# Seven block products instead of eight in a third chunk of each feed-forward part, with weight splits and sums 2048 columns wide

## The chip, the cores and the metric

The kernel runs on one core of a Trainium2 chip, as one program. The core has a matrix engine (TensorE, PE in the profile; its weight loads are listed as PEld), a vector engine (VectorE, DVE), a scalar engine (ScalarE, ACT), GpSimd (POOL) and SyncE (SP), which here issues nearly all loads from memory. Each engine runs its own instructions in their order and waits for others on semaphores. The metric is the device time of one execution in microseconds; smaller is better.

## The reference, cut to what matters

256 tokens of 1024 channels in float32 pass through two stacks. The first has four layers, each a mixer (convolution, pooling, attention, convolution) and a feed-forward part; the second has two layers, each a feed-forward part, a mixer and another feed-forward part. So there are eight feed-forward parts, all of this form (in the second stack the two input matrices are the halves of one):

```
y = rms_norm(x, g)                       # 256 x 1024
f = (silu(y @ w_gate) * (y @ w_up)) @ w_down
x = x + rms_norm(f, g2)                  # halved in the second stack
# w_gate, w_up: 1024 x 2816;  w_down: 2816 x 1024
```

All products have to be as good as float32.

## The kernel before, in words

**Three matmuls for one.** Every weight and activation is split into a hi part, rounded to the matrix engine's reduced float32 format, and a lo part, which is the rest. `mm3` (line 279) is one step: hi by hi, hi by lo, lo by hi, three matmuls of 128 rows, 128 columns of weights from the activation and 512 moving columns (lines 282, 283 and 284). The activations are the stationary side, the split weights the moving one, so the first of the three matmuls reads the weight's hi part, the second its lo part.

**Units.** Weights come as raw tiles of 128 x 2048 float32 (1 MB, one load each). A unit is a raw tile that is to be split: ScalarE copies it to the hi tile (line 229), VectorE subtracts hi from raw into the lo tile (line 190). Each is done in two halves of 1024 columns, so a unit is two copies and two low parts. hi, lo and raw tiles come from one set of 19 buffers (`r8`). In a feed-forward part two hold the split activations and two the split sums of activations, which leaves 15.

**Seven products.** A feed-forward part walks the 2816 hidden columns in six chunks, five of 512 columns and one of 256; in the code they are numbered c = 0 to 5, here they are the first to the sixth. For one chunk, the 1024 input channels fall into two halves, the weights into gate and up, the tokens into two halves of 128: a 2 x 2 block product with blocks b11 (gate, first channels), b12 (up, first), b21 (gate, second) and b22 (up, second). Done plainly (`both`, from line 547, for the second and the fourth chunk) that is eight block products of 4 steps, 32 steps. In the chunks named in `SUMS` (`seven`, from line 582, the third and the fifth) it is done after the scheme of Strassen and Winograd with seven: b11, b21, t1 = b11 + b12, t2 = t1 + b22, b22, t3 = b12 + b22, t4 = t2 + b21, each by an activation block or a sum of activation blocks (made once a part by `x_sums`). That is 28 steps. The sums t1 to t4 are made by VectorE on the raw tiles, in place (`pre_add`, line 170, the additions in line 181): t1, t2 and t4 one after the other on the tile of b11, t3 on the tile of b12. A raw tile can't be added to before the low part of the last unit that was split from it has been issued (line 175). Each of these seven is a unit of its own; a chunk of eight products has four units, since each weight unit serves both token halves.

Between these products stand the steps of the chunk before through `w_down`: 16 steps from two units (d, first and second half; the four calls of `down` in `seven`, interleaved in `both`). The results are taken out of the accumulators by small operations 512 columns wide: in a chunk of seven, three copies and two silu on ScalarE and, on VectorE, an addition for gate 0 (L605), an addition and a product for up 0 (L612, L615), an addition for up 1 (L622) and a product for gate 1 (L630). The hidden values are transposed on the matrix engine (L511) and split (L291 on ScalarE, L292 on VectorE), once for each token half. In a chunk of eight it is L566 and L571 instead of those five.

**What sets the order.** A planner writes the instructions of all engines in one order. `tick` is called after each step and calls `split_step` (line 196), which issues at most the next half unit. It does nothing while its own estimate of VectorE's backlog is over 1.5 steps (`vector`, line 156: one step for 640 columns, with 60 columns added for each operation). Units are taken strictly in order. Before it splits unit i it tries the sum of unit i+1 (lines 206 to 210). It stops, and flushes the low parts that are still to be issued, when unit i is too far ahead of the products (`ahead`), when `limit` units are split and not used up, or when fewer than two buffers are free. Otherwise the low part of a half is issued when the next half has been copied (`flush(1)`). A product whose unit isn't split yet forces it (`need`, `force=True`). `load_step` issues the load of the next raw tile when more than two buffers are free and fewer than three loaded tiles are waiting.

Of the kernel before, what the change touches and what calls it, by code (L numbers as in the profile page):

```python
# [25 lines left out]


ORD = "VQKvco"
SUMS = (2, 4)


class Slots:
# [18 lines left out]
class Core:  # L51
    def __init__(self, ctx, tc, I, out):
        self.tc, self.nc, self.I, self.out = tc, tc.nc, I, out
        P = lambda name, **kw: ctx.enter_context(tc.tile_pool(name=name, bufs=1, **kw))
        sb = P("sb")
        self.sb = sb
        self.r8 = Slots(sb, "r8_", 19, W8, F32R)
        self.r2 = Slots(sb, "r2_", 6, 512, F32R)
        self.f2 = Slots(sb, "f2_", 10, 512, F32)
        self.gn = Slots(sb, "gn_", 2, D, F32)  # L60
        self.ps = Slots(P("ps", space=PSUM), "ps_", 8, 512, F32)
        self.dram = P("dram", space=DRAM)
        self.small_pool = sb
        self.n_small = 0
        self.later = []
        self.ticks = 0
        self.tasks = []
        self.pieces = []
        self.n_dma = self.n_split = 0
        self.sub = 0  # L70
        self.cur, self.ahead = -1, 2
        self.limit = 6
        self.live = 0
        self.raw, self.hl, self.xt = {}, {}, {}
        self.units, self.lows = [], deque()
        self.begun, self.waiting, self.n_low = set(), 0, 0
        self.uses, self.summed = [], set()
        self.vector_until = 0.0
        self.z = {}
        self.raw_max = 3  # L80
        self.spare = 2
        self.reserve = 0
        self.hold = 0
        self.rr, self.nr = {}, {}
        self.pre_gains = deque()
        self.gains, self.gq = deque(), deque()
# [83 lines left out]
    def pre_add(self, i):  # L170

        src, first = self.units[i]
        if first is None or i in self.summed:
            return True
        if src not in self.raw or first not in self.raw or any(self.units[j][0] == src for j in range(self.n_low, i)):
            return False
        self.begin(src)
        self.begin(first)
        a, b = (self.view(self.raw[n], src) for n in (src, first))
        for sl in (slice(0, 2), slice(2, 4)):  # L180
            self.nc.vector.tensor_tensor(out=a[:, sl], in0=a[:, sl], in1=b[:, sl], op=ALU.add)  # L181
            self.vector(1024)
        self.used(first)
        self.summed.add(i)
        return True

    def flush(self, keep=0):
        while len(self.lows) > keep:
            lo, raw, hi, eng, i, last = self.lows.popleft()
            eng.tensor_tensor(out=lo, in0=raw, in1=hi.bitcast(F32), op=ALU.subtract)  # L190
            self.vector(1024)
            if last:
                self.n_low = i + 1
                self.used(self.units[i][0])
# [1 line left out]
    def split_step(self, force=False, eng=None):  # L196
# [27 lines left out]
            self.begin(src)  # L224
        hi, lo = (self.view(t, src) for t in self.hl[i])
        k = hi.shape[1]
        sl = slice(0, k // 2) if self.sub == 0 else slice(k // 2, k)
        raw = self.view(self.raw[src], src)[:, sl]
        self.nc.scalar.copy(out=hi[:, sl], in_=raw)  # L229
        self.lows.append((lo[:, sl], raw, hi[:, sl], eng or self.nc.vector, i, self.sub == 1))  # L230
        self.flush(1)
        self.n_split += self.sub
        self.sub ^= 1
        self.load_step()
        return True

# [258 lines left out]
    def ffn(self, plan, half, nxt):  # L495
        G, Dn = plan
        nc = self.nc
        self.limit, self.reserve, self.ahead = 7, 2, 4
        self.join(self.xt[0])
        xT, rr = self.xT, {0: self.rr[0]}  # L500
        acc = {}
# [190 lines left out]
        for c in range(1, 5):  # L692
# [7 lines left out]
            if c == 3 and nxt == "pool":  # L700
                self.band = self.r8.get(F32)
                nc.sync.dma_start(out=self.band[:, 0:1568], in_=self.band_dram)
        self.ahead = 2
        down(4, 0)
        self.limit, self.ahead = 6, 4
        gate_up(5, 0)
# [1024 lines left out]
```

## Time and profile before

| | us |
|---|---|
| median of 3 runs | 2119.83 (2119.67 to 2119.86) |
| profiled execution | 2119.03 |
| its span, first to last instruction | 2116.5 |
| PE busy | 2090.4 |
| VectorE busy | 1559.2 |
| ScalarE busy | 1211.7 |
| mean granted clock of TensorE, as a share of full speed | 0.999 |

The profile is of one execution. Its times count from the first instruction, so a place in it is given by its microsecond. Matmuls are pipelined and a record of one overlaps the next (0.40 us long, 0.23 us from start to start); the same holds, for less than a tenth of a microsecond, for the operations of VectorE and ScalarE. So the work of an engine is counted here from start to start. In a row, "x5" is five instructions of one form one after the other, "[1.11 <-ACT r L229]" is 1.11 us in which the engine stood before it and what ended that: here ScalarE's line 229. Tile names are without their numbers: r is any buffer of weights or activations, ps an accumulator, f a buffer of 512 columns.

### The profile page before, as it was taken

The numbers are of one execution on the slowest core, as the hardware profiler recorded it, in microseconds if no ns is written. First come the engines' busy times: TensorE is split into PE (matmuls) and PEld (weight loads), VectorE is DVE, ScalarE is ACT, GpSimd is POOL, SyncE is SP. The second block draws the span as 40 slices with busy tenths as digits, with TensorE's granted clock in tenths as the row PEclk, the third lists the DMA queues.
The fourth block names the chain that finished last, engine by engine and source line by source line (L and its number), as shares of the span: only waits on it lengthen the run. The fifth ranks groups of instructions, "written<-read, shape, count | busy, mean of one in ns | idle before, by whom it ended". The sixth has DMA issues, their size and how long they took to land. (4 is left out here: it accounts for less than half of the span.)

```text
span 2116.5 us, 24989 instructions
## 1 busy us (share of the span) xinstructions
PE 2090.4 (99%) x9653; PEld 1688.8 (80%) x9653; DVE 1559.2 (74%) x2016; ACT 1211.7 (57%) x1742; POOL 76.9 (4%) x130
## 2 busy tenths in 40 slices
PE   9999999999999999999999999999999999999998
PEld 6877777888888788887888887878888888787887
DVE  6678678875677776688877774787778776479775
ACT  5566455655665455556555456775556555667553
POOL 1000000000000000000000001010000001000000
PEclk9999999999999999999999999999999999999999
DMA  8556544555444564545555464344564545344442
GB/s 299 192 176 222 185 170 173 205 184 207 140 168 171 189 238 161 187 169 199 206 184 182 152 236 156 120 150 171 207 227 160 209 183 177 133 165 160 179 165 94
DMA packets 175622, 383.74 MB, mean 181 GB/s; under 512 B 10428, under 2 KB 29116, under 8 KB 175504
## 3 DMA queue, kind: packets, MB, share of 16 engines
q1 hardware_dynamic: 172592, 372.04, 49.5%
q0 software_dynamic: 2624, 9.58, 1.3%
q8 instruction: 76, 1.25, 0.2%
q10 hardware_dynamic: 288, 0.52, 0.1%
q14 instruction: 42, 0.34, 0.0%
HBM read 380.28 MB, written 1.84 MB: 181 GB/s over the span
## 5 line engine op out<-in xcount | busy, mean ns | idle before, releaser
L282 PE MATMUL ps<-r,r 128*128 128x512 f32 (+2 forms) x2752 | 1103.0, 401 | 3.6 <-ACT r L291 2.5
L283 PE MATMUL ps<-r,r 128*128 128x512 f32 (+2 forms) x2752 | 1082.0, 393 | 5.3 <-DVE r L190 3.9
L284 PE MATMUL ps<-r,r 128*128 128x512 f32 (+2 forms) x2752 | 1083.0, 394 | 3.1 <-DVE r L292 3.0
L190 DVE TENSOR_TENSOR r<-r,r 128x1024 fp32r<-128x1024 f32 (+1 forms) x797 | 934.2, 1217 | 164.5 <-ACT r L229 161.1
L229 ACT CAST r<-r 128x1024 fp32r<-128x1024 f32 x798 | 791.7, 1043 | 386.7 <-DVE r L181 160.7
L284 PEld LDWEIGHTS ps<-r,r 128*128 128x128 f32 (+1 forms) x2752 | 515.6, 187 | 128.7 <-DVE r L292 9.3
L283 PEld LDWEIGHTS ps<-r,r 128*128 128x128 f32 (+1 forms) x2752 | 516.7, 188 | 120.4 <-DVE r L190 8.6
L282 PEld LDWEIGHTS ps<-r,r 128*128 128x128 f32 (+1 forms) x2752 | 516.8, 188 | 116.0 <-ACT r L291 3.2
L181 DVE TENSOR_TENSOR r<-r,r 128x1024 f32<-128x1024 f32 x128 | 150.9, 1220 | 61.7 <-DMA r<-in_ffn_w_in_dram 31.8
L291 ACT CAST r<-ps 128x512 fp32r<-128x512 f32 (+1 forms) x108 | 59.9, 554 | 150.3 <-PE ps L511 142.1
L292 DVE TENSOR_TENSOR r<-ps,r 128x512 fp32r<-128x512 f32 (+1 forms) x108 | 69.6, 647 | 88.2 <-ACT r L291 88.2
L571 DVE SCALAR_TENSOR_TENSOR f<-ps,rr,f 128x512 f32<-128x512 f32 x32 | 23.9, 748 | 70.0 <-PE ps L284 70.0
L291 ACT CAST r<-f 128x512 fp32r<-128x512 f32 x84 | 51.4, 619 | 37.3 <-DVE f L376 22.2
L312 POOL TENSOR_TENSOR st<-st,c_mhalf 128x1 f32<-128x1 f32 x28 | 15.9, 569 | 1547.2 <-DVE st L311 1546.8
L316 ACT ACTIVATE c_junk<-x 128x512 bf16<-128x512 f32 x56 | 35.3, 631 | 54.8 <-DVE x L349 53.9
L292 DVE TENSOR_TENSOR r<-f,r 128x512 fp32r<-128x512 f32 x84 | 57.6, 709 | 5.6 <-ACT r L291 3.5
L511 PEld LDWEIGHTS ps<-c_ident,f 128*128 128x128 f32 x352 | 44.3, 140 | 13.0
L511 PE MATMUL ps<-c_ident,f 128*128 128x128 f32 x352 | 54.0, 272 | 0.0
L376 DVE TENSOR_TENSOR f<-ps,c_pre 128x512 f32<-128x512 f32 x52 | 33.7, 686 | 22.7 <-PE ps L302 22.1
L349 DVE SCALAR_TENSOR_TENSOR x<-f,st,x 128x512 f32<-128x512 f32 x56 | 39.6, 749 | 2.5 <-POOL st L312 0.9
L316 ACT ACTIVATE c_junk<-ps 128x512 bf16<-128x512 f32 x52 | 31.0, 597 | 17.0 <-PE ps L284 16.2
L341 DVE TENSOR_TENSOR f<-ps,gn 128x512 f32<-128x512 f32 x52 | 35.5, 683 | 6.7 <-ACT c_junk L316 6.7
(193 smaller groups left out, 933.8 us busy)
## 6 DMA issues: line engine op xcount, KB each, us to landing
r<-in_ffn_w_in_dram SPq DMA_DIRECT2D x80, 1024.0 KB, 5.4
r<-in_ffn_w_down_dram SPq DMA_DIRECT2D x44, 1024.0 KB, 6.3
r<-in_ffn_w_out_dram SPq DMA_DIRECT2D x44, 1024.0 KB, 7.1
r<-in_ffn_w_gate_dram SPq DMA_DIRECT2D x40, 1024.0 KB, 5.1
r<-in_ffn_w_up_dram SPq DMA_DIRECT2D x40, 1024.0 KB, 5.3
r<-in_mix_w_in_dram SPq DMA_DIRECT2D x28, 1024.0 KB, 5.0
r<-in_conv_w_in_dram SPq DMA_DIRECT2D x22, 1024.0 KB, 5.8
r<-in_attn_w_qkv_dram SPq DMA_DIRECT2D x12, 1024.0 KB, 5.1
```

The source lines that it names most:

```text
L181: self.nc.vector.tensor_tensor(out=a[:, sl], in0=a[:, sl], in1=b[:, sl], op=ALU.add)
L190: eng.tensor_tensor(out=lo, in0=raw, in1=hi.bitcast(F32), op=ALU.subtract)
L229: self.nc.scalar.copy(out=hi[:, sl], in_=raw)
L282: mm(out=out, lhsT=x[0], rhs=w[0], start=first, stop=False, skip_group_check=more)
L283: mm(out=out, lhsT=x[0], rhs=w[1], start=False, stop=False, skip_group_check=more)
L284: mm(out=out, lhsT=x[1], rhs=w[0], start=False, stop=last, skip_group_check=more)
L291: self.nc.scalar.copy(out=hi, in_=src)
L292: self.nc.vector.tensor_tensor(out=lo, in0=src, in1=hi.bitcast(F32), op=ALU.subtract)
L316: self.nc.scalar.activation(out=self.junk[:, 0:src.shape[-1]], in_=src, func=ACTF.Square, scale=scale, accum_out=acc)
L341: mul = lambda n: nc.vector.tensor_tensor(out=mg[n], in0=src[n], in1=g[:, n * 512:(n + 1) * 512], op=ALU.mult)
L349: nc.vector.scalar_tensor_tensor(out=xs, in0=mg[n], scalar=r, in1=xs, op0=ALU.mult, op1=ALU.add)
L511: nc.tensor.transpose(out=b[:, j * 128:(j + 1) * 128], in_=s[:, j * 128:(j + 1) * 128], identity=self.ident)
```

## The change

The fourth chunk (c = 3) joins `SUMS`, so the third, fourth and fifth chunks are all done with seven products; the order of loads and units of the fourth follows from the same code. `pre_add` makes a sum with one addition of 2048 columns instead of two of 1024. A new flag `whole` is set at the start of each feed-forward part and cleared after its fifth chunk; while it is set, a unit that is begun by the planner, and not forced by a product, is split with one copy and one low part of 2048 columns. A forced unit is still split in two halves. The estimate of VectorE's backlog counts the real width.

```diff
@@ -26,7 +26,7 @@
 
 
 ORD = "VQKvco"
-SUMS = (2, 4)
+SUMS = (2, 3, 4)
 
 
 class Slots:
@@ -76,6 +76,7 @@
         self.begun, self.waiting, self.n_low = set(), 0, 0
         self.uses, self.summed = [], set()
         self.vector_until = 0.0
+        self.whole = False
         self.z = {}
         self.raw_max = 3
         self.spare = 2
@@ -177,9 +178,8 @@
         self.begin(src)
         self.begin(first)
         a, b = (self.view(self.raw[n], src) for n in (src, first))
-        for sl in (slice(0, 2), slice(2, 4)):
-            self.nc.vector.tensor_tensor(out=a[:, sl], in0=a[:, sl], in1=b[:, sl], op=ALU.add)
-            self.vector(1024)
+        self.nc.vector.tensor_tensor(out=a, in0=a, in1=b, op=ALU.add)
+        self.vector(2048)
         self.used(first)
         self.summed.add(i)
         return True
@@ -188,7 +188,7 @@
         while len(self.lows) > keep:
             lo, raw, hi, eng, i, last = self.lows.popleft()
             eng.tensor_tensor(out=lo, in0=raw, in1=hi.bitcast(F32), op=ALU.subtract)
-            self.vector(1024)
+            self.vector(raw.shape[1] * raw.shape[2])
             if last:
                 self.n_low = i + 1
                 self.used(self.units[i][0])
@@ -224,13 +224,15 @@
             self.begin(src)
         hi, lo = (self.view(t, src) for t in self.hl[i])
         k = hi.shape[1]
-        sl = slice(0, k // 2) if self.sub == 0 else slice(k // 2, k)
+        whole = self.whole and self.sub == 0 and not force
+        sl = slice(0, k) if whole else slice(0, k // 2) if self.sub == 0 else slice(k // 2, k)
         raw = self.view(self.raw[src], src)[:, sl]
         self.nc.scalar.copy(out=hi[:, sl], in_=raw)
-        self.lows.append((lo[:, sl], raw, hi[:, sl], eng or self.nc.vector, i, self.sub == 1))
+        self.lows.append((lo[:, sl], raw, hi[:, sl], eng or self.nc.vector, i, whole or self.sub == 1))
         self.flush(1)
-        self.n_split += self.sub
-        self.sub ^= 1
+        if not whole:
+            self.sub ^= 1
+        self.n_split += self.sub == 0
         self.load_step()
         return True
 
@@ -496,6 +498,7 @@
         G, Dn = plan
         nc = self.nc
         self.limit, self.reserve, self.ahead = 7, 2, 4
+        self.whole = True
         self.join(self.xt[0])
         xT, rr = self.xT, {0: self.rr[0]}
         acc = {}
@@ -701,6 +704,7 @@
                 self.band = self.r8.get(F32)
                 nc.sync.dma_start(out=self.band[:, 0:1568], in_=self.band_dram)
         self.ahead = 2
+        self.whole = False
         down(4, 0)
         self.limit, self.ahead = 6, 4
         gate_up(5, 0)
```

## Rows read from the trace of the kernel before

**Rows 1.** The page, part 1: engine, busy us (share of the span), instructions.

```profile
PE 2090.4 (99%) x9653; PEld 1688.8 (80%) x9653; DVE 1559.2 (74%) x2016; ACT 1211.7 (57%) x1742; POOL 76.9 (4%) x130
```

**Rows 2.** Waits, matmuls and weight loads: who waited for whom, us, times, longest.

```profile
PE ps L283 <- DVE r L190: 3.9, 7, 1.3
...
PEld ps L283 <- DVE r L190: 8.6, 12, 1.7
```

**Rows 3.** Windows, fifth part: PE, PEld, DVE, ACT, POOL busy (instructions); clock, DMA, GB/s.

```profile
1106.03:1140.29 34.26, 34.26 (x154) 27.72 (x152) 24.56 (x26) 15.46 (x19) 0.00 (x0) 1.00 0.43 148
1140.29:1171.87 31.58, 31.58 (x144) 25.67 (x142) 28.98 (x29) 23.31 (x27) 0.00 (x0) 1.00 0.57 205
1171.87:1206.40 34.53, 34.46 (x154) 27.69 (x152) 22.00 (x21) 12.55 (x14) 0.00 (x0) 1.00 0.49 178
1206.40:1237.98 31.58, 31.58 (x144) 25.66 (x143) 28.95 (x29) 23.31 (x27) 0.00 (x0) 1.00 0.58 207
```

**Rows 4.** Timeline, matmuls, third chunk: start, us, engine, line, what, [idle before].

```profile
1140.29 0.48 PE L282 MATMUL ps<-r,r 128*128 128x512 f32 x1
...
1157.46 0.40 PE L282 MATMUL ps<-r,r 128*128 128x512 f32 x1
1157.69 0.40 PE L283 MATMUL ps<-r,r 128*128 128x512 f32 x1
...
1171.87 0.39 PE L282 MATMUL ps<-r,r 128*128 128x512 f32 x1
```

**Rows 5.** Timeline, VectorE, third chunk.

```profile
1141.19 0.69 DVE L292 TENSOR_TENSOR r<-ps,r 128x512 fp32r<-128x512 f32 x1 [1.33 <-ACT r L291]
1142.14 1.23 DVE L190 TENSOR_TENSOR r<-r,r 128x1024 fp32r<-128x1024 f32 x1 [0.25 <-ACT r L229]
...
1148.81 0.68 DVE L605 TENSOR_TENSOR f<-ps,f 128x512 f32<-128x512 f32 x1
1149.41 1.21 DVE L190 TENSOR_TENSOR r<-r,r 128x1024 fp32r<-128x1024 f32 x1
1151.74 1.23 DVE L190 TENSOR_TENSOR r<-r,r 128x1024 fp32r<-128x1024 f32 x1 [1.11 <-ACT r L229]
...
1155.15 5.76 DVE L190 TENSOR_TENSOR r<-r,r 128x1024 fp32r<-128x1024 f32 x5
...
1161.55 0.75 DVE L615 SCALAR_TENSOR_TENSOR f<-f,rr,f 128x512 f32<-128x512 f32 x1
1162.22 0.68 DVE L622 TENSOR_TENSOR f<-ps,f 128x512 f32<-128x512 f32 x1
1162.82 6.89 DVE L190 TENSOR_TENSOR r<-r,r 128x1024 fp32r<-128x1024 f32 x6
```

**Rows 6.** Timelines, VectorE (first row) and ScalarE, around the start of the third chunk.

```profile
1134.57 2.36 DVE L181 TENSOR_TENSOR r<-r,r 128x1024 f32<-128x1024 f32 x2 [2.07 <-DMA r<-in_ffn_w_in_dram]
...
1135.91 2.11 ACT L229 CAST r<-r 128x1024 fp32r<-128x1024 f32 x2 [10.50 <-DVE r L181]
1140.57 0.59 ACT L291 CAST r<-ps 128x512 fp32r<-128x512 f32 x1 [2.55 <-PE ps L511]
1141.05 2.00 ACT L229 CAST r<-r 128x1024 fp32r<-128x1024 f32 x2
```

**Rows 7.** Timeline, first chunk of the fifth part, its fourth unit.

```profile
1088.70 5.79 ACT L229 CAST r<-r 128x1024 fp32r<-128x1024 f32 x6
...
1090.46 5.77 DVE L190 TENSOR_TENSOR r<-r,r 128x1024 fp32r<-128x1024 f32 x5
...
1091.74 0.19 PEld L283 LDWEIGHTS ps<-r,r 128*128 128x128 f32 x1 [0.33 <-DVE r L190]
```

**Rows 8.** Windows, third and fifth chunk of the first part.

```profile
168.20:201.20 33.00, 31.92 (x144) 25.62 (x142) 27.55 (x28) 22.28 (x27) 0.00 (x0) 1.00 0.62 223
236.70:268.80 32.10, 31.94 (x143) 25.61 (x142) 26.61 (x27) 21.09 (x25) 0.00 (x0) 1.00 0.63 225
```

**Rows 9.** Windows, the start.

```profile
10.00:20.00 10.00, 9.07 (x36) 7.29 (x37) 8.23 (x11) 6.35 (x14) 2.27 (x2) 0.83 0.86 290
```

## The prediction

> **What bounds the kernel now.** I read the page's busy shares first, then the waits of the matrix engine, then the stretches of one feed-forward part, then its timelines. The busy shares show PE at 99% and DVE at 74% [rows 1]: the matrix engine sets the time, and the vector engine looks as if it had a quarter of the span to spare. The waits agree: over the whole run the matmuls of line 283, the first that read a low part, waited 3.9 us for VectorE, and their weight loads 8.6 us [rows 2]. So a matmul less is time gained, as long as the weights are split in time.
>
> The average hides two kinds of stretch. I take the fifth feed-forward part, which starts at 1081.85. Its chunks of eight products (second and fourth) last 34.26 and 34.53 us with VectorE busy 24.56 and 22.00; its chunks of seven (third and fifth) last 31.58 with VectorE busy 28.98 and 28.95 [rows 3]. A chunk of seven leaves VectorE 2.6 us, a chunk of eight 10 to 12. The kernel now alternates the two, and what the one overdraws the other pays back.
>
> **How much lead is left.** In the third chunk VectorE starts at 1141.19 and is nearly gapless until 1162.82, where the fourth chunk's first split begins [rows 5]. The first half of unit t3's low part ends at 1152.97, and its second, the first of the five low parts from 1155.15, at 1156.4; t3's product starts at 1157.46 and wants the second half two steps (1.4 us) later [rows 4, 5]. That is 2.5 us of margin, the least of the chunk. The fourth chunk's first low part is complete at 1162.82 + 2 x 1.14 = 1165.1, against its use at 1171.87: a lead of 7 us. Today a chunk of eight follows and rebuilds it. After the change a chunk of seven follows, and then another.
>
> **The change, part by part.**
>
> *One product less in the fourth chunk.* It drops 4 steps of 3 matmuls. Starts are 0.23 us apart [rows 4], so 12 x 0.232 = 2.8 us; the two stretches measured differ by 34.53 - 31.58 = 2.95 [rows 3]. I take 2.95 a part, bounds 2.7 and 3.1; eight parts: -23.6 us. It lies on PE and is real if nothing waits.
>
> *What VectorE gets for it.* Three more weight units to split and four sums, so 9 splits and 4 sums in each of three chunks, beside seven small operations: five of 0.60 and two of 0.67 by their spacing [rows 5], 4.3 us. A 1024-wide low part follows the one before by (5.76 - 1.22)/4 = 1.135 us, a 512-wide operation by 0.60 [rows 5]. So 512 more columns cost 0.535, and 2048 wide should take 1.135 + 1.07 = 2.21, against 2.27 for two halves. Bounds 2.14 (0.07 less again) and 2.27. Thirteen of them are 28.7 us; with the small ones 33.0 us in a chunk in which PE needs 31.6. Already without any idle time VectorE is 1.4 us a chunk too slow.
>
> *What the width costs.* In halves the second half of a sum runs while ScalarE copies the first: the sums start at 1134.57, the first copy at 1135.91, 0.11 after the first half [rows 6]; the low part follows with no wait for the copy. With one sum, one copy and one low part each waits for the whole of the one before. A copy 1024 wide takes (5.79 - 1.05)/5 = 0.95 by spacing [rows 7], one 512 wide 0.48 [rows 6], so 2048 should take 1.88 by spacing and 1.97 by its record. From the earliest next start on VectorE (0.08 before the sum's record ends) to the low part: 0.08 + 0.11 + 1.97 + 0.04 = 2.2 us. The 0.04 is the gap from the first of the copies from 1141.05, with 1.05, to the low part of 1142.14 [rows 5, 6]. This hole comes at t1 and at t2, where it can't be filled: t2 is summed in place on the tile from which t1 was summed, so its sum waits for t1's low part (line 175), and the planner takes units strictly in order, so nothing but a small operation can stand there. t3 and t4 are summed one unit ahead and have no hole. Two holes a chunk, 0 to 2.2 us each; I take the whole, since the durations are measured and only the order is inferred, but in the fifth chunk I let small operations stand in the holes at no cost.
>
> *Third to fourth chunk, added up on VectorE's queue in the fifth part.* Start 1141.19; three small 1.8, then seven wide (sum t3, first down unit, b22, sum t4, t3, second down unit, t4) 15.5: 1158.5. Then 1.3 for the half-0 up value, b11 2.2, up value of half 1 0.6 (its product ends at 1160.3), b21 2.2, sum t1 2.2: 1167.0. Hole 2.2, t1 2.2, small 0.6, sum t2 2.2, hole 2.2, t2 2.2, small 0.7: 1179.3. Sum t3 2.2, down unit 2.2, small 0.6, b22 2.2, small 0.6, sum t4 2.2, t3 2.2: 1191.5. PE wants it 17.4 us into the chunk (17.17 in the third chunk, and 0.23 because the hi part alone feeds the first matmul): 1171.87 + 17.4 = 1189.3 [rows 4]. Late by 2.2, so PE stands 2.2 us.
>
> *Fourth to fifth chunk.* From t3 to the next t3: 13 wide 28.7, small ones outside the holes 3.1, holes 4.4: 36.2 against 31.6 of PE. Late by another 4.6. Together 6.8 us a part, 54 us in eight. Bounds: without holes VectorE is 2.2 us early in the fourth chunk and never late: 0. With 2.27 for a wide one and everything else as above: 8.7. I stay at 6.8.
>
> Here the Trainium skill has two rules side by side, in "Perfetto Trace Analysis", section "Optimizing Scalar/DVE Operations": larger operations help an engine that is saturated, since each pays some 60 ns of access on VectorE, and breaking operations up helps one that is not saturated but makes bubbles on others. The rows agree with the first (0.06 us saved a pair); by that rule alone the sum would have no holes and come out some 54 us lower. The second rule speaks against this change, and the holes above are what it would mean here.
>
> *The width at the start of a part.* In the first chunk the fourth unit is split late: its copies start at 1088.70, its first half low part at 1090.46, and the weight load at 1091.74 already waited 0.33 us for it [rows 7]. One whole low part would start after a copy of 1.97, at 1090.7, and end at 1093.0 instead of 1091.6: 1.3 us later, less 0.1 that today's second half costs. I take 1.2 a part, 9.6 in all; bounds 0 (the unit is forced and stays in halves) and 2.2.
>
> *The first part.* Its chunks of seven already take 33.00 and 32.10 us instead of 31.58 [rows 8], because VectorE has more to do there. I add 2 us, bounds 0 and 4.
>
> *The rest costs nothing.* Bytes and number of weight loads are the same, and ScalarE needs 9 x 1.9 + 4 = 21 us in a chunk of 31.6. The evacuations of the seven products replace those of the eight and are in the 4.3 us.
>
> **The sum.** -23.6 + 54.4 + 9.6 + 2 = +42.4 us. The profiled execution took 2119.03 us, 0.8 under the median of the runs shown, so 2119.0 + 42.4 = 2161.4; against the median it would be 2162.2. I say 2162.
>
> **Rivals.**
>
> *Faster: the holes are filled.* If the planner, short of a free buffer, flushes b11's low part before it takes b21, t1 is summed one unit early and b21's low part stands in the first hole. Buffers are short: 15 of the 19 are left for weights, and a chunk of seven holds four raw tiles. Against it: with VectorE late, PE frees buffers first. With both holes covered nothing waits: -23.6 and 0 to 9.6, so 2095 to 2105; with one of two filled, half the hole time goes (2.2 us in the fourth chunk, 2.2 in the fifth): 6.8 - 4.4 = 2.4 a part, and with the start 2119.0 + 8 x (2.4 + 1.2 - 2.95) = 2124, less where the start costs less. I put the rival at 2100, the middle of the first two.
>
> *Slower still: the raw weights come late.* The sum of t2 waited 2.07 us for its load [rows 6]. If in the fourth and fifth chunks b22 finds a buffer only when the third chunk's last down unit is done, VectorE waits there too: 2 x 2.07 x 8 = 33 us more, 2195. Against it: late VectorE means that loads have had longer.
>
> *The clock.* Standing still can lower the granted clock: in the stretch from 10 to 20 us it is 0.83, the only one of those shown below 1.00 [rows 9], so 3.4 us went at the lower of 1.2 and 2.4 GHz, which costs 1.7. After each of some sixteen stalls: 27 us more, 2189. Against it: the waits of the first part left its chunks at 1.00 [rows 8]. The Trainium skill, "TensorE: Matmul & The Clock Gate", section "Why this matters for your kernels", has the rule that idle gaps between bursts of matmuls bring the clock down; the trace neither shows nor excludes it for gaps of 2 us amid dense work.
>
> **How the numbers follow.** The forecast has 0.58, the filled holes 0.27 for faster and 0.05 for about even (one hole in two filled and a little less at the start), late loads 0.07, the clock 0.03. What a measurement of this kernel can tell from no change is 0.2%, 4.2 us. So faster 0.27, same 0.05, slower 0.68. The range reaches down into the filled holes, to 2102, and up to 2185, which is 8 x (8.7 + 2.2 - 2.95) + 2 above 2119: the wide operations at 2.27 and the start at 2.2. The likeliest case's own range is 2135 to 2185; its lower end is wide operations of 2.14, which take 2.2 of the 6.8 away, and a start that costs nothing: 8 x (4.6 - 2.95) + 2.
>
> **What would show it.** Right: a fourth-chunk stretch of 31.6 us of matmuls that lasts 33 to 35, a fifth of 35 to 37, matmul waits for line 190 of some 50 us in all instead of 3.9, VectorE waiting 2.1 us for the copy at t1 and t2, a wide low part of 2.2 by spacing. Wrong: chunks of 31.6 us three times in a row, or a first chunk no longer than today's.

## The result, and the profile after

The changed kernel takes 2195.59 us (median of 4 runs, 2193.85 to 2196.38) against 2119.85 for the kernel before: 1.0356 times as long, 95% interval 1.0344 to 1.0369. The forecast was 2162 in a range of 2102 to 2185. The direction was right, the time lies above the range.

Lines have moved a little: the low part is still L190, the weight copy L229 is L230, the second matmul L283 is L285, and L601, L628, L630 and L292 are L604, L631, L633 and L294. The page, part 1, of the kernel after:

```profile
PE 2100.8 (96%) x9557; PEld 1678.4 (77%) x9557; DVE 1672.2 (76%) x1761; ACT 1235.0 (56%) x1519; POOL 76.9 (4%) x130
```

96 matmuls are gone, yet PE's share fell from 99 to 96% [rows 1]: it waits. The waits of the kernel after (who for whom: us in total, times, longest):

```profile
PEld ps L285 <- DVE r L190: 70.4, 62, 2.3
...
PE ps L285 <- DVE r L190: 47.5, 36, 2.0
...
PE ps L284 <- ACT f L604: 25.0, 26, 1.5
```

The matmuls' wait for low parts, 3.9 us before [rows 2], is 47.5. The second wait, for L604 (the copies of the products out of the accumulators), is new. Where it happens, by the windows of the fifth part, first to fifth chunk (columns as in [rows 3]):

```profile
1116.00:1141.35 25.35, 24.14 (x109) 19.03 (x109) 21.20 (x25) 15.62 (x20) 2.21 (x4) 1.00 0.45 152
1141.35:1175.59 34.24, 34.24 (x152) 27.71 (x152) 23.21 (x18) 14.84 (x13) 0.00 (x0) 1.00 0.41 148
1175.59:1207.17 31.58, 31.58 (x143) 25.70 (x142) 29.52 (x19) 18.65 (x15) 0.00 (x0) 1.00 0.56 200
1207.17:1242.91 35.74, 32.64 (x141) 25.33 (x141) 30.58 (x19) 19.12 (x15) 0.00 (x0) 1.00 0.48 177
1242.91:1281.66 38.75, 35.26 (x141) 27.38 (x141) 30.09 (x20) 21.20 (x18) 0.00 (x0) 0.91 0.47 163
```

The second and third chunks last as long as before [rows 3]. The first is 1.17 us longer (24.18 before), the fourth, which lost four steps, 1.21 longer instead of 2.95 shorter, the fifth 7.17 longer. From this stretch, free of waits, of 31.58 to those of 35.74 and 38.75 the stall is 4.2 and 7.2 us: 11.3 a part. The eight parts are longer by 8.2 to 11.8 us each, which accounts for the 75 us.

What happens on VectorE is seen at the border of the third to the fourth chunk. VectorE, kernel after (start, us, line, [idle before and what ended it]):

```profile
1200.14 2.29 DVE L181 TENSOR_TENSOR r<-r,r 128x2048 f32<-128x2048 f32 x1
1204.45 2.29 DVE L190 TENSOR_TENSOR r<-r,r 128x2048 fp32r<-128x2048 f32 x1 [2.03 <-ACT r L230]
1206.66 0.69 DVE L294 TENSOR_TENSOR r<-ps,r 128x512 fp32r<-128x512 f32 x1
1207.26 2.28 DVE L181 TENSOR_TENSOR r<-r,r 128x2048 f32<-128x2048 f32 x1
1212.15 0.75 DVE L633 SCALAR_TENSOR_TENSOR f<-f,rr,f 128x512 f32<-128x512 f32 x1 [2.61 <-ACT f L631]
1212.82 2.28 DVE L190 TENSOR_TENSOR r<-r,r 128x2048 fp32r<-128x2048 f32 x1
1215.02 2.28 DVE L181 TENSOR_TENSOR r<-r,r 128x2048 f32<-128x2048 f32 x1
1217.22 2.28 DVE L190 TENSOR_TENSOR r<-r,r 128x2048 fp32r<-128x2048 f32 x1
1219.43 0.68 DVE L608 TENSOR_TENSOR f<-ps,f 128x512 f32<-128x512 f32 x1
1221.37 0.69 DVE L294 TENSOR_TENSOR r<-ps,r 128x512 fp32r<-128x512 f32 x1 [1.26 <-ACT r L293]
```

ScalarE at the same place:

```profile
1209.63 1.91 ACT L230 CAST r<-r 128x2048 fp32r<-128x2048 f32 x1 [4.73 <-DVE r L181]
1211.44 0.68 ACT L631 ACTIVATE f<-ps,rr 128x512 f32<-128x512 f32 x1
1212.02 3.70 ACT L230 CAST r<-r 128x2048 fp32r<-128x2048 f32 x2
```

L181 is the sum of t1, then of t2, and at 1215.02 of t3. The hole before t1's low part, 2.03, is the wait of 2.1 that was forecast. In the hole before t2's stands a small operation (L633), but it doesn't fill the hole: VectorE stands 2.61 us before it, for the silu of L631, which is on ScalarE's queue behind the very copy (1209.63) that t2's low part needs. t2's low part starts 5.56 us after its sum, of which 2.2 are the sum. At 1221.37 another small operation (L294, the low part of a hidden value) adds a wait of 1.26.

### The profile page after: what moved, and what is told of

It reads as the page before. It is cut to its first block, busy times and chain, and to the rows that moved or that the text cites. A ratio compares the mean times of both kernels' runs of the same rounds, so it can differ in the third digit from the quotient of the medians.

```text
span 2191.9 us, 24366 instructions
## 1 busy us (share of the span) xinstructions
PE 2100.8 (96%) x9557; PEld 1678.4 (77%) x9557; DVE 1672.2 (76%) x1761; ACT 1235.0 (56%) x1519; POOL 76.9 (4%) x130
## 4 chain that ended last, share of the span: by engine, by line
PE 70%; DVE 19%; issue 5%; ACT 4%; DMA 1%; POOL 1%; DVEq 0%; SPq 0%; POOLq 0%; ACTq 0%
PE ps L285 21%; PE ps L286 21%; PE ps L284 21%; DVE r L190 11%; DVE r L181 5%; ACT r L230 2%; PE ps L304 2%; PE ps L514 1%; ACT r L293 1%; DVE r L294 1%; PE ps L1334 1%; ACT c_junk L318 1%; PE ps L1410 1%; ACT f L631 0%; DVE f L378 0%
## 5 line engine op out<-in xcount | busy, mean ns | idle before, releaser
L285 PE MATMUL ps<-r,r 128*128 128x512 f32 (+1 forms) x2720 | 1079.1, 397 | 50.2 <-DVE r L190 47.5
L284 PE MATMUL ps<-r,r 128*128 128x512 f32 (+1 forms) x2720 | 1098.6, 404 | 26.5 <-ACT f L604 25.0
L190 DVE TENSOR_TENSOR r<-r,r 128x2048 fp32r<-128x2048 f32 (+2 forms) x550 | 964.4, 1787 | 162.0 <-ACT r L230 159.9
L286 PE MATMUL ps<-r,r 128*128 128x512 f32 (+1 forms) x2720 | 1074.5, 395 | 0.1
L230 ACT CAST r<-r 128x2048 fp32r<-128x2048 f32 (+2 forms) x551 | 805.3, 1501 | 394.1 <-DVE r L181 289.2
L285 PEld LDWEIGHTS ps<-r,r 128*128 128x128 f32 x2720 | 514.0, 189 | 178.9 <-DVE r L190 70.4
L284 PEld LDWEIGHTS ps<-r,r 128*128 128x128 f32 x2720 | 514.2, 189 | 150.3 <-ACT f L604 38.1
L286 PEld LDWEIGHTS ps<-r,r 128*128 128x128 f32 x2720 | 512.9, 189 | 120.7 <-DVE r L294 3.9
L181 DVE TENSOR_TENSOR r<-r,r 128x2048 f32<-128x2048 f32 x96 | 219.4, 2285 | 22.6 <-DMA r<-in_ffn_w_in_dram 11.8
L294 DVE TENSOR_TENSOR r<-ps,r 128x512 fp32r<-128x512 f32 (+1 forms) x108 | 69.7, 648 | 91.4 <-ACT r L293 91.1
L294 DVE TENSOR_TENSOR r<-f,r 128x512 fp32r<-128x512 f32 x84 | 57.5, 709 | 4.2 <-ACT r L293 2.1
L633 DVE SCALAR_TENSOR_TENSOR f<-f,rr,f 128x512 f32<-128x512 f32 x24 | 18.0, 750 | 41.8 <-ACT f L631 41.8
L611 ACT ACTIVATE f<-f,rr 128x512 f32<-128x512 f32 x24 | 17.4, 724 | 52.2 <-DVE f L608 52.2
L604 ACT COPY f<-ps 128x512 f32<-128x512 f32 x72 | 41.0, 584 | 7.7 <-PE ps L286 7.7
```

Source lines behind the costliest of these rows:

```text
L181: self.nc.vector.tensor_tensor(out=a, in0=a, in1=b, op=ALU.add)
L284: mm(out=out, lhsT=x[0], rhs=w[0], start=first, stop=False, skip_group_check=more)
L285: mm(out=out, lhsT=x[0], rhs=w[1], start=False, stop=False, skip_group_check=more)
L286: mm(out=out, lhsT=x[1], rhs=w[0], start=False, stop=last, skip_group_check=more)
L294: self.nc.vector.tensor_tensor(out=lo, in0=src, in1=hi.bitcast(F32), op=ALU.subtract)
L604: nc.scalar.copy(out=f[n], in_=b)
```

## The experiments

Times are medians; each ratio is to the kernel before in the same session, with its 95% interval.

**1. The third seven alone, in halves.**

```diff
 # the kernel before
-SUMS = (2, 4)
+SUMS = (2, 3, 4)
```

> Only the third chunk of seven is added to the kernel before; splits and sums stay in halves of 1024 columns. Theory A (VectorE is the bound, and it is the width that puts holes in its queue at t1 and t2: the sum, the copy and the low part of 2048 columns stand one after the other, and small operations that wait for ScalarE's queue lengthen the hole): without holes VectorE needs 13 x 2.27 + 4.3 = 33.8 us a chunk against 31.6, and is about in time up to the fifth chunk; each part gains 2.95 us and loses 0 to 3 again, so 2096 to 2116, middle 2108. Rival B (three chunks of seven in a row overload VectorE by themselves and the width is neutral but for the first chunk): the fourth and fifth chunks stall by 4 and 7 us as after the change, so 2185.

2186.15 us, 1.0311 (1.0296 to 1.0327). My theory A was that the wide operations make the holes and halves do without; it fell, and the time is rival B's 2185. The windows of its fifth part, third to fifth chunk:

```profile
1173.21:1204.78 31.57, 31.57 (x143) 25.69 (x142) 28.43 (x28) 19.52 (x23) 0.00 (x0) 1.00 0.56 200
1204.78:1238.86 34.08, 32.05 (x141) 25.43 (x140) 31.41 (x32) 19.18 (x23) 0.00 (x0) 1.00 0.57 196
1238.86:1278.01 39.15, 33.35 (x142) 25.13 (x140) 30.86 (x30) 19.48 (x23) 0.00 (x0) 1.00 0.50 179
```

The stall is there without one wide operation (2.5 + 7.6), and with the clock at 1.00. Two groups of its page (busy, mean ns of one | idle before, what ended most of it):

```profile
L283 PE MATMUL ps<-r,r 128*128 128x512 f32 (+1 forms) x2720 | 1076.1, 396 | 73.1 <-DVE r L190 71.6
L282 PE MATMUL ps<-r,r 128*128 128x512 f32 (+1 forms) x2720 | 1092.6, 402 | 4.6 <-ACT f L601 1.9
```

In this kernel the matmuls wait 71.6 us for low parts and 1.9 for the copies of L601; in the kernel after it was 47.5 and 25.0, together 72.5. By these totals the wait for those copies, behind wide weight copies on ScalarE's queue, took the place of a wait for VectorE and added next to nothing; the third experiment tests it.

**2. The width alone.**

```diff
 # the kernel after
-SUMS = (2, 3, 4)
+SUMS = (2, 4)
```

> Only the width is added to the kernel before; the fourth chunk keeps eight products. Theory A: the first chunk gets 1.2 us longer in each part (9.6 in all, a little more in the last part), the chunks of seven keep their 31.6 because the chunk of eight before each of them gives the lead back; 2129 to 2131. Rival B: the same. Rival C (the wide copies stand in front of the evacuations on ScalarE, and the matmuls wait for line 604 in any chunk of seven): 25 us of such waits in 24 chunks, so some 17 in 16: 2145 or more.

2129.42 us, 1.0044 (1.003 to 1.0058): +9.6. The first chunk of the fifth part takes 25.41, the chunks of seven stay at 31.6. The width costs 1.2 us at the start of each part and nothing in a seven that follows an eight.

**3. Is it VectorE's load or ScalarE's?** Each sum adds 128 of its 2048 columns.

```diff
 # the kernel after
-        self.nc.vector.tensor_tensor(out=a, in0=a, in1=b, op=ALU.add)
+        self.nc.vector.tensor_tensor(out=a[:, 0, 0:128], in0=a[:, 0, 0:128], in1=b[:, 0, 0:128], op=ALU.add)
```

> The kernel after, but each of the four sums of a chunk adds only 128 of its 2048 columns; the other columns of t1 to t4 are the unsummed blocks, so the result is another. The order is the same, and ScalarE's work is the same. Theory A: VectorE has 4 x 2.1 us less in a chunk, 24.6 us against 31.6, so no chunk of seven stalls: 2119 - 23.6 + 9.6 = 2106, 2104 to 2112. Rival C (ScalarE's queue holds up the matmuls): its copies and evacuations are as many as before, so most of the waits for line 604 stay, and the time stays above 2140.

2102.76 us, 0.9917 (0.9897 to 0.9936), a little under theory A's 2104. The windows of its fourth and fifth chunks in the fifth part:

```profile
1162.50:1194.00 31.50, 31.50 (x142) 25.56 (x141) 23.77 (x19) 18.88 (x15) 0.00 (x0) 1.00 0.56 201
1194.00:1225.80 31.80, 31.80 (x142) 25.55 (x141) 23.05 (x19) 20.13 (x16) 0.00 (x0) 1.00 0.58 199
```

ScalarE does as much as before, and in these chunks TensorE waits for nothing. The planner still counts 2048 columns a sum, and from the first to the fifth chunk of all eight parts the instructions of VectorE and of ScalarE stand in the same order as in the kernel after, so VectorE's load alone is changed. The stall needs the sums' time on VectorE. The matmuls' wait for L604 goes from 25.0 to 0.9 us with it.

**4. Wide from the second chunk on.**

```diff
 # the kernel after, ffn
-        self.whole = True          # ahead of the first chunk
...
+        self.whole = True          # after gate_up(0, 1)
```

> The kernel after, but the first chunk of each part is split in halves as before; the width begins with the second chunk. If the 1.2 us by which each first chunk grew come from the one wide split of its fourth unit, the time falls by 9.6 us and up to 2 more in the last part: 2184 to 2187. If they come from elsewhere (the sum of the fourth chunk, later loads), it stays at 2195.

2182.8 us, 1.0294 (1.0279 to 1.031). The first chunk is back at 24.19, and the whole is 12.8 us shorter, a little more than the 9.6 to 11.6 expected. Against halves everywhere (first experiment) the wide operations are worth 3.4 us: after the first chunk the width is about neutral for the whole time.

**5. Two sevens in a row.**

```diff
 # the kernel before
-SUMS = (2, 4)
+SUMS = (2, 3)
```

> The kernel before with its two chunks of seven side by side (third and fourth); the fifth has eight products; all in halves. As many matmuls, splits and sums as before, only the neighbourhood is changed. Theory D (VectorE's account: a chunk of seven costs it as much work as PE has time, and each us in which it stands idle in such a run of chunks comes out as a stall; a chunk of eight pays back): the fourth chunk stalls by 2.5 us as in the run with three chunks in halves, the fifth not; 8 x 2.5 above 2120, 2136 to 2144. Rival (the stall comes from where the fifth chunk stands, at the hand-over to the sixth, not from a row of sevens): no more than 2 us a part in the fourth, and the time within 2120 to 2128.

2144.86 us, 1.0118 (1.0103 to 1.0133), just over what was expected. The number of matmuls is the same as before; the order alone costs 25 us. In the fifth part the fourth chunk takes 34.10 instead of 31.6, the chunk of eight behind it 0.9 more than the 34.2 that such a chunk takes without waits, and the sixth 0.4 more. The window of the fourth chunk:

```profile
1184.77:1218.87 34.10, 32.05 (x142) 25.42 (x141) 31.39 (x32) 21.08 (x25) 0.00 (x0) 1.00 0.61 214
```

**6. Two sums on GpSimd.**

```diff
 # the first experiment, pre_add
+            if i in self.on_pool:      # t3 and t4
+                self.nc.gpsimd.tensor_tensor(out=a[:, sl], in0=a[:, sl], in1=b[:, sl], op=ALU.add)
```

> Three chunks of seven in halves, with the sums for t3 and t4 (issued one unit ahead) on GpSimd instead of VectorE, which has 4 x 1.14 = 4.5 us less in a chunk. GpSimd took 2.36 us for a 1024-wide subtraction in the kernel before, so 9.4 us a chunk, beside VectorE. Theory D: about 11 us less work in the 88 us that VectorE took from the start of the third chunk to t3 of the fifth, against 8.3 us by which it was late: hardly a stall is left, 2094 to 2106. Rival E (the two engines get in each other's way in the buffers, and VectorE's operations get longer beside GpSimd's): the saving is eaten up, 2140 to 2190, and VectorE's 1024-wide records grow well beyond 1.22 us. Rival F (ScalarE's order, not VectorE's load): no more than 15 us better than the 2186 in halves.

2264.94 us, 1.0678 (1.0662 to 1.0694): the rival was right, and by more than it said. Groups of this run (busy, mean ns of one):

```profile
L196 DVE TENSOR_TENSOR r<-r,r 128x1024 fp32r<-128x1024 f32 x841 | 1114.3, 1371 | 149.9 <-ACT r L235 145.6
...
L185 POOL TENSOR_TENSOR r<-r,r 128x1024 f32<-128x1024 f32 x96 | 300.4, 3151 | 748.6 <-DMA r<-in_ffn_w_in_dram 284.3 <-DMA r<-in_ffn_w_up_dram 186.9 <-PE ps L290 108.8
```

A low part of 1024 columns, 1217 ns on average in the first experiment, takes 1371. 841 of them are 130 us more of VectorE, while the sums taken away were 117. The average mixes two kinds. Two low parts on VectorE, and the two GpSimd additions beside them (start, us):

```profile
1209.23 6.19 DVE L196 TENSOR_TENSOR r<-r,r 128x1024 fp32r<-128x1024 f32 x2
1207.65 6.69 POOL L185 TENSOR_TENSOR r<-r,r 128x1024 f32<-128x1024 f32 x2 [1.16 <-DVE r L196]
```

The 93 low parts that lie for more than half of their time beside a GpSimd addition take 2588 ns on average, the 744 that touch none 1219. VectorE's operations that read an accumulator (L298) keep their 0.68 us beside one. Other operations with two inputs in the buffers grow too (L636, a product, 1980 ns on average instead of 752), so VectorE lost more than it was spared. TensorE's waits here are for copies out of the accumulators (L607, 114.1 us, 34 times; 4.1 for low parts), which stand on ScalarE's queue behind weight copies. The Trainium skill, "SBUF — State Buffer", section "Who interferes with whom", states that a VectorE instruction with two inputs in SBUF contends with a GpSimd instruction that reads SBUF; the 2588 against 1219 ns agree.

**7. The gate of half 1 later,** so that L630 stands behind t2's low part and not in its hole.

```diff
 # the first experiment
-                self.spawn(gate1(), 1)
+                self.spawn(gate1(), 5)
```

> Three chunks of seven in halves; the last gate value of a chunk (line 628 on ScalarE, line 630 on VectorE) is issued five steps after its product instead of one, and its transposes move back with it. Nothing else. Theory D, idle time counts: VectorE no longer waits some 0.6 us for line 628 in each of the fourth and fifth chunks, nor some 1.3 us for line 291 behind line 608 in the fourth; 1 to 2.5 us a part, so 2166 to 2178. Rival (only the load counts): 2186 as before, within 3.

2191.49 us, 1.0339 (1.0321 to 1.0356): a miss. In the fourth chunk of the fifth part t2's low part does start 2.39 us after its sum began, instead of 3.64 in the first experiment, so the hole is closed. Nothing is gained by it: VectorE's idle time is the same over the stretch (table below).

**8. Halves for the sums and their units, wide for the rest.**

```diff
 # the fourth experiment
-        whole = self.whole and self.sub == 0 and not force
+        whole = self.whole and self.sub == 0 and not force and first is None
 # and the sums in two halves
```

> The width from the second chunk on, but the sums and the units t1 to t4 in halves; 2048 columns only for the units without a sum. If the holes of the wide sums at t1 and t2 are what is lost (two of 2.0 to 2.5 us in each of the fourth and fifth chunks, less what the halves cost, 1 us), the stall of 11.2 us a part falls to 4 to 6: 2130 to 2143. Rival (VectorE loses as much in other places when the holes are gone, as in the run in halves): 2175 to 2186.

2235.29 us, 1.0545 (1.0529 to 1.0561): a miss of both theories, and the worst of the kinds of width. Two of its waits:

```profile
PE ps L286 <- DVE r L191: 71.4, 68, 2.4
...
DVE f L615 <- PE ps L287: 25.8, 8, 4.0
```

I read the second row as a loop, which no run separates: VectorE waits, once a part and up to 4.0 us, at an addition for a product of TensorE that is late because VectorE was late, and every low part behind it waits along.

**What the eight runs have in common.** From the start of the third chunk to t3's product (its second step) in the fifth, mean of the third to eighth part, in us. TensorE alone needs 81.0 there, as the last two rows show; the stall is what the span has above that:

| kernel | span | VectorE busy | VectorE idle | stall |
|---|---|---|---|---|
| after | 92.2 | 80.9 | 11.3 | 11.2 |
| 1, halves | 88.2 | 79.9 | 8.3 | 7.2 |
| 4, wide from the second chunk | 92.2 | 80.8 | 11.3 | 11.2 |
| 7, gate later | 88.8 | 80.4 | 8.4 | 7.8 |
| 8, mixed | 94.2 | 79.4 | 14.7 | 13.2 |
| 6, GpSimd | 102.8 | 96.9 | 5.9 | 21.8 |
| 9, two sums narrow (below) | 80.9 | 73.4 | 7.5 | 0 |
| 10, two sums by DMA (below) | 81.0 | 73.7 | 7.3 | 0 |

Idle is the span less busy, so the stall is busy plus idle less 81.0 by arithmetic; that proves no cause. What the table shows is the size: in the kernel after VectorE's work alone is TensorE's time, so whatever makes it stand idle leaves no room. The third experiment shows the other side: with 60.7 busy VectorE stands idle 20.1 us in the same stretch, and the stall is 0. Halves have 4 us less stall than wide ones here, and give it back after the window (in the fifth part the fifth chunk lasts 39.15 instead of 38.75, the sixth, counted to the first step of the next part, 30.97 instead of 29.54). What should help is less work on VectorE. Three more runs test that.

**9. The dose: two sums of four narrow.**

```diff
 # the first experiment, pre_add
-            self.nc.vector.tensor_tensor(out=a[:, sl], in0=a[:, sl], in1=b[:, sl], op=ALU.add)
+            n = 64 if i in self.narrow else 512      # t3 and t4
+            self.nc.vector.tensor_tensor(out=a[:, sl, 0:n], in0=a[:, sl, 0:n], in1=b[:, sl, 0:n], op=ALU.add)
-            self.vector(1024)
+            self.vector(2 * n)
```

> Three sevens in halves (the first experiment), with the additions of the third and fourth sum narrowed to 128 of 1024 columns a half, on VectorE as before; the result differs by what these two sums leave out. It takes some 4 us of VectorE in each seven-product chunk and nothing else: no other engine gets work, no queue changes. Theory (VectorE's own work and idle time make the stall: 79.9 busy + 8.3 idle against TensorE's 81.0 in the stretch from the third chunk to the fifth): busy falls by about 10 us over the stretch, the stall of 7.2 goes, and the time is 2095 to 2108, 15 to 24 below the kernel before. Rival (the stall is made by the chain of the order, copies behind evacuations and small operations, which is unchanged): 2150 to 2185.

2100.47 us, 0.9911 (0.9896 to 0.9926): the theory's figure. With some four microseconds less of VectorE in a chunk the first experiment's 2186 becomes 2100. The fifth chunk of the fifth part, 39.15 us in the first experiment, is now:

```profile
1192.71:1224.94 32.23, 31.66 (x142) 25.39 (x140) 28.77 (x32) 22.98 (x27) 0.00 (x0) 1.00 0.59 207
```

One thing more changes than the expectation says: the planner counts the narrower sums (the last line of the edit), so it issues VectorE's and ScalarE's instructions in another order than in the first experiment. Load and order change together here, and in the next run too; it is the third experiment that changes the load alone.

**10. The same two sums by transfers, nothing left out.**

```diff
 # the first experiment, pre_add; tried for t3 and t4 as soon as the last low part of their tile is issued
+        if i in self.acc and i not in self.summed:
...
+            self.nc.gpsimd.dma_start(out=self.view(self.raw[src], src), in_=self.acc[i], accum_op=ALU.add)
```

> Three sevens in halves, with the whole third and fourth sum made by transfers: GpSimd's queue issues a DMA that adds the 1 MB block from memory onto the block in its buffer, as soon as the last low part (or sum) that reads the buffer is done; nothing is left out. VectorE loses 4 x 1.22 = 4.9 us in each such chunk. Theory: if the adding transfer is as quick as the plain ones (5 to 7 us from issue to landing), it lies beside the splits of two or three units (4.5 us each) and the stall goes: 2095 to 2108. Rival (the adding transfer is the new wait: it reads its destination too, is issued by another queue, and adds 2 MB a chunk to DMA engines that are half busy; above some 10 us from issue to landing the fourth sum's copy is late, and each us more is a us of stall): 2130 to 2200.

2093.74 us (2093.29 to 2093.95), 0.9878 (0.9862 to 0.9895): 1.2% below the kernel before and 4.6% below the one after, with the whole computation, and 1 us under the theory's range. Its windows, third to fifth chunk of the fifth part:

```profile
1127.43:1159.05 31.62, 31.62 (x143) 25.66 (x142) 27.83 (x28) 20.72 (x25) 1.28 (x1) 1.00 0.91 256
1159.05:1190.58 31.53, 31.53 (x142) 25.58 (x141) 30.03 (x30) 21.55 (x26) 2.55 (x2) 1.00 0.86 255
1190.58:1222.06 31.48, 31.48 (x142) 25.59 (x141) 28.71 (x29) 24.01 (x28) 1.29 (x1) 1.00 0.92 283
```

and two rows of its DMA issues (KB each, median us from issue to landing):

```profile
r<-in_ffn_w_in_dram SPq DMA_DIRECT2D x80, 1024.0 KB, 5.7
...
r<-in_ffn_w_in_dram POOLq DMA_DIRECT2D x24, 1024.0 KB, 9.9
```

Three sevens in a row at 31.6 with no stall; so it is in the other parts too, but for the third chunk of the second part (34.50). An adding transfer (POOLq) takes 9.9 us where a plain load takes 5.7, and the DMA engines go from a share of 0.57 [rows 3] to 0.9; both are hidden.

**11. The control: the same transfers with two sevens.**

```diff
 # the tenth experiment
-SUMS = (2, 3, 4)
+SUMS = (2, 4)
```

> The kernel before (sevens in the third and fifth chunk) with the third and fourth sum made by adding transfers, as the control for the experiment beside it. Theory: TensorE waits for little in the kernel before (3.9 us for low parts in all), so VectorE's relief is worth nothing: 2117 to 2121. If the adding transfers are late or slow the others, 2125 to 2170 here too, and then the difference between this run and the one beside it is what the third seven costs with them.

2114.88 us, 0.9979 (0.997 to 0.9989), 2 us below what was expected: the chunk of eight between the sevens takes 34.1 to 34.3 in all parts, where in the kernel before it takes 34.2 to 35.5. So the third seven with this relief is worth 2114.88 - 2093.74 = 21.1 us, 2.64 a part.

**12. Four sevens in a row.**

```diff
 # the tenth experiment
-SUMS = (2, 3, 4)
+SUMS = (1, 2, 3, 4)
```

> Seven products in the second chunk too (second to fifth), halves, third and fourth sum of each by adding transfers. Theory (the stall is VectorE's work and idle time against TensorE's time, and with the adding transfers there is room in every chunk): each part loses another 34.2 - 31.6 = 2.65 us, 21 in all, so 2070 to 2080. Rival (the second chunk follows too closely on the first: VectorE makes the first sums, and the sums of the activations x, while the first chunk's units are still split, and the first product that needs the latter waits): 3 to 8 us come back in each part, 2093 to 2135.

2142.72 us, 1.0105 (1.0088 to 1.0122), slower than the rival's 2135. The second chunk does take 31.5 to 31.9 in the third to eighth part (40.5 and 37.3 in the first two), so the place that the rival named is not where most is lost: there the third to fifth chunks take 32 to 36. Waits of this run, then its adding transfers:

```profile
ACT r L244 <- DVE r L193: 237.7, 63, 5.4
...
PEld ps L297 <- ACT f L616: 48.8, 35, 3.4
...
ACT r L244 <- DMA r<-in_ffn_w_in_dram: 44.8, 17, 4.3
...
PE ps L297 <- ACT f L616: 33.9, 31, 3.0
```

```profile
r<-in_ffn_w_in_dram POOLq DMA_DIRECT2D x7, 1024.0 KB, 12.8
```

(The last row is of the fifth part.) TensorE now waits for the copies out of the accumulators (L616), which stand on ScalarE's queue behind weight copies (L244), and these for VectorE's sums (L193) and for data. Which of the two weighs more I can't tell from this run; no experiment separated them.

## Why the prediction was wrong in its size

*The product less* was forecast at 2.95 us a part. Without stalls it measures 2.64 (eleventh against tenth), just under its lower bound of 2.7; the stretch of 34.53 [rows 3] is longer than the 34.1 to 34.3 of the same chunk in the eleventh.

*The lead and its loss* was right: without a chunk of eight in between, VectorE is late in the fourth chunk and later in the fifth, and nothing is lost in the third. Experiments 1, 3, 5, 9 and 10 show it: sevens in a row make the stall, and less work on VectorE removes it.

*The wide operation* at 2.21 was right (1215.02 to 1217.22 is 2.20), *the first chunk* too (1.2 forecast, 1.17 measured; 9.6 in all forecast and measured in the second experiment). *The first part's* 2 us more did not come: it grew by 8.6, no more than the others. Nor does its reason stand in the rows: VectorE is busy 27.55 and 26.61 us in those chunks [rows 8], less than the 28.98 of the fifth part [rows 3].

*The step that failed is the size of the stall*: the forecast 2.2 in the fourth chunk and "another 4.6" in the fifth were 4.2 and 7.2. The two assumptions behind it were that small operations cost their spacing of 0.60 or 0.67 wherever they stand, and "in the fifth chunk I let small operations stand in the holes at no cost". The rows of the fifth part show the opposite. A small operation in a hole needs a result of ScalarE, and ScalarE's queue is at that moment at the wide copy that makes the hole, so the small one runs after the hole and pushes the low part back further. By rows of the kernel after, in the fourth chunk t2's low part starts 5.56 us after its sum began, where 4.4 were forecast; 0.7 of that was counted as a small one behind it, which leaves 0.5. The wait of L294 at 1221.37 adds 1.26. Together 1.7 of the 1.95 that are missing. In the fifth chunk t1's low part starts 5.39 us after its sum and t2's 5.57, against 4.4 each: 2.2 of the missing 2.55:

```profile
1239.38 2.28 DVE L181 TENSOR_TENSOR r<-r,r 128x2048 f32<-128x2048 f32 x1
1244.17 0.69 DVE L294 TENSOR_TENSOR r<-ps,r 128x512 fp32r<-128x512 f32 x1 [2.51 <-ACT r L293]
1244.77 2.28 DVE L190 TENSOR_TENSOR r<-r,r 128x2048 fp32r<-128x2048 f32 x1
1247.09 2.29 DVE L181 TENSOR_TENSOR r<-r,r 128x2048 f32<-128x2048 f32 x1
...
1252.66 2.29 DVE L190 TENSOR_TENSOR r<-r,r 128x2048 fp32r<-128x2048 f32 x1
```

This account is read from rows: no run moved the small operations of the wide kernel, and in halves, where one was moved out of its hole, the idle time came back elsewhere (seventh experiment). So what went wrong in the sum is shown, but not that another place for these operations would have saved it. Eight parts times 4.5 us are 36; the 2 of the first part and some tenths go the other way, and the forecast was 33.5 short. The bound of 8.7, and with it the range, had the wide operations dearer and left the idle time as it was; the idle time of VectorE was what needed a bound. One sign came out by luck: matmuls waiting "some 50 us" for line 190. It is 47.5, but of a stall of 90 us in eight parts instead of 54, and 25.0 more went to the wait for L604, which the forecast didn't have.

*"The rest costs nothing"* was right of ScalarE's load, 19 to 21 us a chunk, and of its evacuations (first experiment); it was the order of its queue, with the small operations, that cost.

*A second error lay behind it*, which the time doesn't show: I blamed the holes on the width. Halves stall as well (first experiment), with 8.3 us of idle time of their own. The Trainium skill's rule in "Perfetto Trace Analysis", section "Optimizing Scalar/DVE Operations", that larger operations help a saturated engine, is worth 3.4 us here after the first chunk (fourth against first experiment). The section's other rule, on bubbles, shows in the first chunk (1.2 us a part) and in the stretch of the table, where halves stall 7.2 us instead of 11.2, which they give back behind it.

*The rivals.* The holes were not filled. "Late loads" has the measured time, 2195, by luck, with a wrong mechanism: VectorE's sums waited 62 us for loads in the kernel before and 23 in the one after. The clock did fall (below), but the first experiment stalls nearly as long (10.1 us against 11.3 in the fifth part) where it stays at 1.00.

## What to carry to other kernels

When two engines alternate between loaded and light stretches, add up the second engine's work over the whole run of loaded stretches, not its share of the span: once that sum reaches the first engine's time, there is no room for its idle time, from whatever order, and a forecast needs a bound on that too. None of the orders and widths tried here ended the stall (7.2 to 13.2 us in the table); taking work off the engine did (here two sums of four, by adding transfers on a queue with room). By the rows of the kernel after, a small operation placed in a hole only fills it if what it needs is not queued behind what makes the hole.

## What the runs showed of the hardware

In the kernel after, the clock fell after short waits amid dense work. Three windows of the kernel after, in the fifth chunk of the fifth part (the granted clock is the third number from the end):

```profile
1245.00:1253.90 8.90, 7.01 (x29) 5.08 (x28) 6.25 (x4) 4.43 (x4) 0.00 (x0) 1.00 0.55 226
1253.90:1260.70 6.80, 5.70 (x15) 4.57 (x16) 6.80 (x6) 3.82 (x5) 0.00 (x0) 0.50 0.00 0
1260.70:1270.00 9.30, 8.80 (x38) 6.84 (x37) 7.81 (x5) 7.80 (x5) 0.00 (x0) 1.00 0.68 226
```

and matmuls before and in it:

```profile
1252.49 0.50 PE L284 MATMUL ps<-r,r 128*128 128x512 f32 x1 [0.98 <-ACT f L604]
1255.01 0.80 PE L285 MATMUL ps<-r,r 128*128 128x512 f32 x1 [2.01 <-DVE r L190]
```

One matmul between two waits of 1 and 2 us, and the clock stood at half, 1.2 GHz, for 6.8 us; it fell 0.9 us into the second wait. Such a stretch came eight times between the start and the end of this execution, for 3.4 or 6.8 us each. Here it cost little, while TensorE was waiting for VectorE anyway: the fifth chunk of the sixth part has no such stretch and takes 38.73, as long as the 38.75 here. In the first chunk of the eighth part it did cost, 28.93 against 27.32 in the sixth.

The kernel before has one such stretch, at its start, with the same kind of waits ahead of it; the prediction had that window's clock, but not these waits. Two of its matmuls and the window that follows:

```profile
9.01 0.49 PE L282 MATMUL ps<-r,r 128*128 128x512 f32 x1 [1.88 <-ACT r L291]
10.93 0.78 PE L283 MATMUL ps<-r,r 128*128 128x512 f32 x1 [1.42 <-POOL r L190]
11.00:14.40 3.40, 3.40 (x8) 2.55 (x9) 3.40 (x6) 2.66 (x5) 0.97 (x1) 0.50 1.05 399
```

Waits alone don't tell when it falls: in the first experiment matmuls waited 70 times for low parts, up to 1.5 us, and the clock fell twice between the start and the end.

Beside GpSimd's additions VectorE's low parts took 2588 ns instead of 1219, while its operations that read an accumulator kept 0.68 us (sixth experiment); in the run with adding transfers from GpSimd's queue the low parts kept 1216 on average (tenth experiment).
